# Attention's two passes taken in turns between heads, on key tiles of their own, and the convolution's edge columns copied on ScalarE

## The chip, the core and the metric

The kernel runs on one core of one Trainium2 chip. The metric is the device time of one execution in microseconds (us), lower is better; the time before is the median of three runs. Engines are named as the profile names them: PE (TensorE, matrix products), PEld (its weight loads), DVE (VectorE), ACT (ScalarE), POOL (GpSimd) and SP (SyncE, whose queue issues most DMAs). PE accumulates in PSUM; everything else works on SBUF tiles or on PSUM banks.

## The reference

One block over 2048 tokens with a model width of 1024, all in float32. Shortened:

```python
h = rms_norm(x, norm_mix_g)
z = h @ w_in                          # u_a, v_a (512 each), q, k, v (512 each), 8 forget logits
out_a = spatial_gating(gelu(u_a), gelu(v_a), ...)      # 128-token blocks
c = cumsum(log_sigmoid(f_logit))                       # per head
s = q @ k.T / 8 + c[t] - c[s]         # 8 heads of 64, s <= t
out_b = softmax(s) @ v
x = x + concat(out_a, out_b) @ w_out
a = rms_norm(x, norm_ffn_g) @ w_up    # 2 x 2816 channels
a = causal_conv3(a, w_conv) + b_conv  # depthwise, over tokens
g, val = split(a)
x = x + (silu(g) * val) @ w_down
out = rms_norm(x, norm_final_g)
```

## The kernel before, in words

**Precision and tiling.** A float32 operand is split into a high part, rounded to the matmul's format (fp32r), and a low part (the difference). A product is then three matmuls: high x high, high x low, low x high (`mm3`, recorded at L212; 24 matmuls of 512 columns for a sum over 1024). The high part of a weight is made by POOL (L151), the low part by DVE (L165). Tokens go in blocks `tb` of 512, two blocks to a half of 1024.

**Stages.** Phase A makes q, k, v, the forget sums and the gated heads. `c_half` multiplies by W_out for the first half, `d_half` does the first half's up-projection and convolution (22 pairs of channel tiles, `f`), `c_late` is W_out for the second half, and then the second half's up-projection and both down-projections follow, in another scheme of products. What `c_half` and `c_late` read of attention has gone through DRAM: `b_mix` writes two heads at a time to `mixh` and `mixl`, and `load_mix(blk)` reads a block of 512 tokens back in eight DMAs, into tiles of the tpool that `d_half` uses for its own input. `load_mix(2)` is issued near the end of `d_half`, `load_mix(3)` in the first part of `c_late`.

**Attention** is a generator, `b_stream`, that runs through 32 pieces: token block 0 to 3, and in each the heads 0 to 7. A piece has two passes. `b_max(h, tb)` makes the scores with queries on the partitions (L777, one matmul of 96 rows) and reduces each to its row minimum on DVE (L780, or L782 on the diagonal), since q was stored negated. `b_mix(h, tb)` makes the scores again with keys on the partitions (L824, L828, and a mask at L826), takes exp on ACT into `e` (L830), splits it into `ph` (ACT, L835) and `pl` (DVE, L836), adds it to `sum` (DVE, L838), and multiplies both parts by v into the PSUM bank `o` (L812, L813; "PV" below). Then come the row sums (L854, L855), and after every odd head the normalisation: `rw` (ACT), its four transposes (L186), `op` (DVE, L863), a split and two DMAs to `mixh` and `mixl`. Each `yield` of the generator is one step: one score matmul with its reduction in `b_max`, one chunk of 128 keys in `b_mix`.

**What sets the order.** Attention fills the other stages: `tick` is called after each matmul of the main work, and after `rate` of them (3.6 in `d_half`) one step of attention is written, with a raised priority. `need(tb)` runs the generator on until a token block is done. From all of this a scheduler makes one fixed order for every engine and every DMA queue; on the chip each engine follows its order and waits on semaphores. `b_stream` writes, for each piece, the whole of `b_max(h, tb)` and then the whole of `b_mix` of the piece before:

```python
t1, turn = yield from self.b_max(h, tb)
if todo:
    yield from self.b_mix(*todo, turn)
    self.done += 1
...
todo = (h, tb, t1, self.b_low(h, tb))
```

`t1` holds q's high part with the forget and maximum rows, `m1` the same for the keys, `m2` and `t2` the rest, `v4` the values. Two `m1` buffers are shared by both passes (`b_keys`); `t2` and `sum` have one buffer each. `turn`, a transpose (L796) and a product on DVE (L797), puts the row maxima into `t1`; it is called at the fourth chunk of the mix before. After the first two channel pairs of `d_half` the pool of `c_half`'s rows is closed and `bx` is opened in its place; `more` is true from there to the end of attention, and `room` then gives some tiles (`e`, `ph`, `pl`, `m2`, `v`) further buffers, marked `+`.

**The convolution** in `d_up`: `a` has 514 columns, two of them from the block before. ACT copies the product from PSUM to columns 2 to 513 (L934) and makes `t` from it with the third tap and the bias (L935); DVE copies the two columns from `halo` to `a` (L936) and the last two of `a` to `halo` (L937), and adds the other two taps (L938, L939).

Of the kernel before, what the change touches and what calls it, by code (L numbers as in the profile page):

```python
# [8 lines left out]
F32 = mybir.dt.float32  # L9
F32R = mybir.dt.float32r  # L10
BF16 = mybir.dt.bfloat16
AF = mybir.ActivationFunctionType
ALU = mybir.AluOpType
# [5 lines left out]
P = 128  # L19
# [16 lines left out]
LAG = 2  # L36
TURN = 3
# [16 lines left out]
def f32(ap):  # L54
    return ap.bitcast(F32)
# [26 lines left out]
class Block:  # L82
# [625 lines left out]
    def b_stream(self, pieces):  # L708

        todo = None  # L710
        for h, tb in pieces:
            if tb >= 2 and not self.ready:
                if todo:
                    yield from self.b_mix(*todo, None)
                    self.done += 1
                    todo = None
                while not self.ready:
                    yield
            t1, turn = yield from self.b_max(h, tb)
            if todo:  # L720
                yield from self.b_mix(*todo, turn)
                self.done += 1
            else:
                turn()
            todo = (h, tb, t1, self.b_low(h, tb))
        yield from self.b_mix(*todo, None)
        self.done += 1

# [14 lines left out]
    def b_keys(self, h, sb, values):  # L743
        hf, sl = sb // 2, slice((sb % 2) * TB, (sb % 2 + 1) * TB)
        self.M1.append(self.M1.pop(0))
        m1 = self.M1[0]
# [9 lines left out]
    def b_low(self, h, tb):  # L756

        t2 = self.til(self.mp, [P, TB], F32R, "t2")
        self.dma(f32(t2), self.qx[tb // 2][h, :, (tb % 2) * TB:(tb % 2 + 1) * TB])
        return t2  # L760
# [41 lines left out]
    def b_mix(self, h, tb, t1, t2, turn):  # L802

        nc, bp, pp = self.nc, self.bp, self.bpp
        po = self.til(pp, [P, TB], F32, "o")
        total = self.til(self.mp, [P, TB], F32, "sum")
# [116 lines left out]
    def d_up(self, f, wg, wv, b):  # L923
# [3 lines left out]
        for ch, (wh, wl) in ((f, wg), (NF + f, wv)):  # L927
# [8 lines left out]
            nc.vector.tensor_copy(a[:, 0:2], self.halo[:, ch, :])  # L936
            nc.vector.tensor_copy(self.halo[:, ch, :], a[:, TB:TB + 2])  # L937
            nc.vector.scalar_tensor_tensor(t, a[:, 1:TB + 1], self.cw1[:, cc], t, op0=ALU.mult, op1=ALU.add)  # L938
            nc.vector.scalar_tensor_tensor(t, a[:, 0:TB], self.cw0[:, cc], t, op0=ALU.mult, op1=ALU.add)  # L939
# [14 lines left out]
    def d_half(self):  # L954

        units = lambda f: [self.load_unit(self.a["w_up"][c], P) for c in (f, NF + f)]
        for f0 in range(0, NF, 2):
# [17 lines left out]
            if not f0:  # L975
# [3 lines left out]
                self.more = True  # L979
    def d_sums(self, i):  # L980
# [581 lines left out]
```

## Time and profile before

| | us |
|---|---|
| median of three runs (2420.01 to 2422.13) | 2421.57 |
| the profiled execution, its own time | 2422.66 |
| its span, from the first to the last instruction | 2420.9 |
| PE busy in the span | 2379.3 |
| DVE busy | 1881.9 |
| ACT busy | 1152.9 |
| POOL busy | 331.3 |

The mean granted TensorE clock is 0.995 of full speed. A matmul's record covers its way through the array, so that records overlap: a matmul of 512 columns is shown with some 0.39 us and the next one starts 0.23 us later. What PE loses is therefore read from the starts of its instructions and from its waits. In the rows of a timeline stand the start, the duration, the engine, line, operation, tiles and shapes, and in brackets the idle time before it with what ended it. In the rows of waits stand the total, the count and the longest. In the rows of groups stand the busy time and the mean duration in ns, then the idle time before them.

### The profile page before, as it was taken

The numbers are of one execution on the slowest core, as the hardware profiler recorded it, in microseconds if no ns is written. First come the engines' busy times: TensorE is split into PE (matmuls) and PEld (weight loads), VectorE is DVE, ScalarE is ACT, GpSimd is POOL, SyncE is SP. The second block draws the span as 40 slices with busy tenths as digits, with TensorE's granted clock in tenths as the row PEclk, the third lists the DMA queues.
The fourth block names the chain that finished last, engine by engine and source line by source line (L and its number), as shares of the span: only waits on it lengthen the run. The fifth ranks groups of instructions, "written<-read, shape, count | busy, mean of one in ns | idle before, by whom it ended". The sixth has DMA issues, their size and how long they took to land.

```text
span 2420.9 us, 32633 instructions
## 1 busy us (share of the span) xinstructions
PE 2379.3 (98%) x11352; PEld 1973.2 (82%) x11352; DVE 1881.9 (78%) x3196; ACT 1152.9 (48%) x1987; POOL 331.3 (14%) x315
## 2 busy tenths in 40 slices
PE   9999999999999999999999999899999999999998
PEld 7888878988787888888878888688888888888887
DVE  5457776776579888998999988598888877857775
ACT  4335655533334444454544445465555455454444
POOL 4014140010232222222221110100000000000001
PEclk9999999999999999999999999899999999999999
DMA  8662625567754444444443464312222228438633
GB/s 278 184 230 94 197 74 171 153 188 247 244 193 151 154 142 153 147 140 158 160 155 121 159 217 152 122 53 95 79 81 85 87 93 313 159 98 296 205 119 123
DMA packets 234518, 379.58 MB, mean 157 GB/s; under 512 B 49944, under 2 KB 109464, under 8 KB 232928
## 3 DMA queue, kind: packets, MB, share of 16 engines
q1 hardware_dynamic: 229312, 353.36, 44.9%
q0 software_dynamic: 5040, 24.12, 2.6%
q8 instruction: 90, 1.47, 0.3%
q14 instruction: 76, 0.62, 0.1%
HBM read 283.82 MB, written 93.72 MB: 156 GB/s over the span
## 4 chain that ended last, share of the span: by engine, by line
PE 79%; DVE 5%; DMA 2%; issue 2%; ACT 2%; POOL 1%; SPq 0%; POOLq 0%; DVEq 0%; ACTq 0%
PE mm L212 35%; PE D L1376 13%; PE A L1174 3%; PE A L1176 3%; PE A L1175 3%; PE o L813 3%; PE o L812 2%; PE s L777 2%; PE s L828 2%; PE s L824 2%; PE B L1175 2%; PE B L1176 2%; PE B L1174 2%; PE C L1174 1%; PE C L1175 1%
## 5 line engine op out<-in xcount | busy, mean ns | idle before, releaser
L212 PE MATMUL mm<-thi,wlo 128*128 128x512 f32 x896 | 352.9, 394 | 0.0
L212 PE MATMUL mm<-thi,whi 128*128 128x512 f32 x896 | 352.1, 393 | 0.5 <-DVE vn L520 0.5
L212 PE MATMUL mm<-tlo,whi 128*128 128x512 f32 x896 | 352.5, 393 | 0.0
L212 PE MATMUL mm<-whi,thi 128*128 128x512 f32 (+2 forms) x768 | 277.4, 362 | 14.3 <-DMA thi<-mixh 8.8
L212 PE MATMUL mm<-wlo,thi 128*128 128x512 f32 (+2 forms) x768 | 276.7, 361 | 1.9 <-DVE wlo L165 1.8
L212 PE MATMUL mm<-whi,tlo 128*128 128x512 f32 (+2 forms) x768 | 275.4, 360 | 1.3 <-DMA tlo<-mixl 1.3
L151 POOL TENSOR_SCALAR whi<-raw 128x1024 fp32r<-128x1024 f32 (+3 forms) x114 | 135.2, 1187 | 909.3 <-PE mm L212 665.9
L212 PEld LDWEIGHTS mm<-thi,whi 128*128 128x128 f32 x896 | 168.8, 188 | 34.5 <-issue 0.9
L212 PEld LDWEIGHTS mm<-tlo,whi 128*128 128x128 f32 x896 | 168.8, 188 | 33.9
L212 PEld LDWEIGHTS mm<-thi,wlo 128*128 128x128 f32 x896 | 168.9, 188 | 33.2
L838 DVE TENSOR_TENSOR sum<-sum,e 128x512 f32<-128x512 f32 (+3 forms) x249 | 163.6, 657 | 20.8 <-ACT e L830 18.2
L212 PEld LDWEIGHTS mm<-whi,thi 128*128 128x128 f32 x768 | 146.1, 190 | 35.8 <-DMA thi<-mixh 9.6
L212 PEld LDWEIGHTS mm<-wlo,thi 128*128 128x128 f32 x768 | 146.1, 190 | 22.5 <-DVE wlo L165 3.1
L212 PEld LDWEIGHTS mm<-whi,tlo 128*128 128x128 f32 x768 | 146.0, 190 | 21.4 <-DMA tlo<-mixl 1.7
L830 ACT ACTIVATE e<-s 128x512 f32<-128x512 f32 (+3 forms) x207 | 105.9, 518 | 114.0 <-PE s L828 64.1
L165 DVE TENSOR_TENSOR wlo<-raw,whi 128x1024 fp32r<-128x1024 f32 (+2 forms) x106 | 134.8, 1274 | 28.0 <-POOL whi L151 27.6
L1376 PE MATMUL D<-wh,xh 128*128 128x512 f32 x368 | 140.8, 389 | 1.2 <-DVE xo L1477 1.2
L1376 PE MATMUL D<-wl,xh 128*128 128x512 f32 x368 | 141.4, 389 | 0.0
L836 DVE TENSOR_TENSOR pl<-e,ph 128x512 fp32r<-128x512 f32 (+3 forms) x195 | 122.2, 632 | 20.5 <-PE o L813 10.7
L1376 PE MATMUL D<-wh,xl 128*128 128x512 f32 x368 | 137.5, 389 | 0.0
L835 ACT ACTIVATE ph<-e 128x512 fp32r<-128x512 f32 (+3 forms) x195 | 104.4, 547 | 42.4 <-PE o L812 29.5
L934 ACT ACTIVATE a<-mm 128x512 f32<-128x512 f32 x88 | 52.4, 596 | 119.5 <-PE mm L212 119.1
(1839 smaller groups left out, 5776.2 us busy)
## 6 DMA issues: line engine op xcount, KB each, us to landing
raw<-in_w_up_dram SPq DMA_DIRECT2D x72, 512.0 KB
m<-kx SPq DMA_DIRECT2D x160, 136.0 KB
x<-act SPq DMA_DIRECT2D x84, 256.0 KB
m<-kx SPq DMA_DIRECT2D x67, 256.0 KB
v<-vd SPq DMA_DIRECT2D x67, 256.0 KB
raw<-in_w_in_dram SPq DMA_DIRECT2D x28, 512.0 KB
raw<-in_w_out_dram SPq DMA_DIRECT2D x24, 512.0 KB
tw<-in_w_down_dram SPq DMA_DIRECT2D x11, 1024.0 KB
```

What stands on the lines that cost most here:

```text
L151: self.cast_ins = self.nc.gpsimd.tensor_scalar(out, in_, 1.0, 0.0, ALU.mult, ALU.add).ins
L165: nc.vector.tensor_tensor(lo, raw, f32(hi), op=ALU.subtract)
L212: self.last_mm = self.nc.tensor.matmul(ps, lhsT=a[k], rhs=b[k], start=i == 0, stop=i == 3 * n - 1).ins
L813: nc.tensor.matmul(po[:, c], lhsT=v, rhs=pl[:, c], start=False, stop=sc == ns - 1)
L830: nc.scalar.activation(e[:, c], ps[:, c], AF.Exp, scale=-1.0)
L835: nc.scalar.activation(ph[:, c], e[:, c], AF.Copy)
L836: nc.vector.tensor_tensor(pl[:, c], e[:, c], f32(ph[:, c]), op=ALU.subtract)
L838: nc.vector.tensor_tensor(total[:, c], total[:, c], e[:, c], op=ALU.add)
L1174: mm(ps, lhsT=xh[:, ks], rhs=yh[:, k, :], start=fresh and k == 0, stop=False, **kw)
L1175: mm(ps, lhsT=xh[:, ks], rhs=yl[:, k, :], start=False, stop=False, **kw)
L1176: mm(ps, lhsT=xl[:, ks], rhs=yh[:, k, :], start=False, stop=k == 3, **kw)
L1376: nc.tensor.matmul(bank[t], lhsT=x[i][:, ts], rhs=w[k], start=fresh and j == 0 and i + k == 0, stop=last and i == 1, **kw)
```

## The change

`b_stream` alternates the two passes once `more` is true: three steps of `b_max` of the next head, then two steps of `b_mix` of the one before, until `b_max` is through; the rest of `b_mix` follows, with `turn` called at its fourth remaining step. The mix pass takes its `m1` tiles from a ring of their own (`M1b`, two tiles in the pool `bx`, filled with their constant rows by four memsets on POOL), and `t2` and `sum` get a second buffer there. `b_low`, the load of `t2`, moves from the end of the mix before into the beginning of `b_mix`. In `d_up` both copies of edge columns go from DVE to ACT; for the first block (b = 0), where the edge is zero, the copy into `a` is left out and the two taps run on 511 and 510 columns.

```diff
--- before.py
+++ after.py
@@ -34,6 +34,7 @@
 AHEAD_B, AHEAD_W = 100, 2000
 WARM = 24
 LAG = 2
+FIRST, SECOND = 3, 2
 TURN = 3
 GATE_LAG = 30
 
@@ -43,7 +44,7 @@
     "x": 4, "st": 4, "ln": 2, "vn": 4, "u": 2, "lns": 8, "fs": 7, "fr": 3,
     "m1": 2, "t1": 2, "m2": 2, "v": 2, "t2": 1, "e": 3, "op": 1, "ph": 2, "pl": 2, "part": 2, "mx": 2, "m8": 2,
     "rr": 2, "rw": 1, "sum": 1,
-    "ar": 4, "a": 2, "t": 4, "ss": 4, "rs": 4, "rstd": 8, "tw": 1, "s0": 1, "va": 2, "e+": 1, "ph+": 2, "pl+": 2, "m2+": 1, "v+": 1,
+    "ar": 4, "a": 2, "t": 4, "ss": 4, "rs": 4, "rstd": 8, "tw": 1, "s0": 1, "va": 2, "e+": 1, "ph+": 2, "pl+": 2, "m2+": 1, "v+": 1, "m1+": 2, "sum+": 1, "t2+": 1,
     "mm": 2, "tp": 2, "dn": 2, "s": 3, "o": 1,
     "y": 1, "sf": 2, "tq": 1, "cv": 2, "ts": 2, "xgP2l": 1, "xgP2h": 1, "xgP1l": 1, "xgP1h": 1, "xsP7l": 1, "xsP7h": 1, "xsP6l": 1, "xsP6h": 1, "xsP5l": 1, "xsP5h": 1, "xsP4l": 1, "xsP4h": 1, "xsP3l": 1, "xsP3h": 1, "pc": 2, "A": 3, "B": 1, "C": 3,
     "wr": 2, "wh": 3, "wl": 3, "xh": 3, "xl": 3, "x11": 9, "wr+": 2, "wh+": 2, "wl+": 2, "xh+": 2, "xl+": 2, "x11+": 2, "x12": 11, "x21": 11, "x22": 11, "xs": 2,
@@ -716,15 +717,44 @@
                     todo = None
                 while not self.ready:
                     yield
-            t1, turn = yield from self.b_max(h, tb)
-            if todo:
-                yield from self.b_mix(*todo, turn)
+            if todo and self.more:
+                first, second = self.b_max(h, tb), self.b_mix(*todo, None)
+                t1 = None
+                while t1 is None:
+                    for _ in range(FIRST):
+                        t1, turn = yield from self.one(first)
+                        if t1 is not None:
+                            break
+                    if t1 is None:
+                        for _ in range(SECOND):
+                            yield from self.one(second)
+                for n, _ in enumerate(second):
+                    if n == TURN:
+                        turn()
+                        turn = None
+                    yield
+                if turn:
+                    turn()
                 self.done += 1
             else:
-                turn()
-            todo = (h, tb, t1, self.b_low(h, tb))
+                t1, turn = yield from self.b_max(h, tb)
+                if todo:
+                    yield from self.b_mix(*todo, turn)
+                    self.done += 1
+                else:
+                    turn()
+            todo = (h, tb, t1)
         yield from self.b_mix(*todo, None)
         self.done += 1
+
+    def one(self, gen):
+
+        try:
+            next(gen)
+        except StopIteration as end:
+            return end.value or (None, None)
+        yield
+        return None, None
 
     def room(self, shape, dt, tag):
 
@@ -742,8 +772,9 @@
 
     def b_keys(self, h, sb, values):
         hf, sl = sb // 2, slice((sb % 2) * TB, (sb % 2 + 1) * TB)
-        self.M1.append(self.M1.pop(0))
-        m1 = self.M1[0]
+        ring = self.M1b if values and self.more else self.M1
+        ring.append(ring.pop(0))
+        m1 = ring[0]
         self.dma(f32(m1[0:68, :]), self.kx[hf][h, 64:132, sl])
         if not values:
             return m1
@@ -755,7 +786,7 @@
 
     def b_low(self, h, tb):
 
-        t2 = self.til(self.mp, [P, TB], F32R, "t2")
+        t2 = self.room([P, TB], F32R, "t2")
         self.dma(f32(t2), self.qx[tb // 2][h, :, (tb % 2) * TB:(tb % 2 + 1) * TB])
         return t2
 
@@ -799,11 +830,12 @@
 
         return t1, turn
 
-    def b_mix(self, h, tb, t1, t2, turn):
+    def b_mix(self, h, tb, t1, turn):
 
         nc, bp, pp = self.nc, self.bp, self.bpp
+        t2 = self.b_low(h, tb)
         po = self.til(pp, [P, TB], F32, "o")
-        total = self.til(self.mp, [P, TB], F32, "sum")
+        total = self.room([P, TB], F32, "sum")
         ns = 4 * tb + 4
         late = []
 
@@ -933,10 +965,13 @@
             cc = slice(ch, ch + 1)
             nc.scalar.activation(a[:, 2:TB + 2], ps, AF.Copy)
             nc.scalar.activation(t, ps, AF.Identity, scale=self.cw2[:, cc], bias=self.cb[:, cc])
-            nc.vector.tensor_copy(a[:, 0:2], self.halo[:, ch, :])
-            nc.vector.tensor_copy(self.halo[:, ch, :], a[:, TB:TB + 2])
-            nc.vector.scalar_tensor_tensor(t, a[:, 1:TB + 1], self.cw1[:, cc], t, op0=ALU.mult, op1=ALU.add)
-            nc.vector.scalar_tensor_tensor(t, a[:, 0:TB], self.cw0[:, cc], t, op0=ALU.mult, op1=ALU.add)
+            if b:
+                nc.scalar.activation(a[:, 0:2], self.halo[:, ch, :], AF.Copy)
+            nc.scalar.activation(self.halo[:, ch, :], a[:, TB:TB + 2], AF.Copy)
+            for n, cw in ((1, self.cw1), (0, self.cw0)):
+                c = slice(0 if b else 2 - n, TB)
+                nc.vector.scalar_tensor_tensor(t[:, c], a[:, n + c.start:n + TB], cw[:, cc], t[:, c],
+                                               op0=ALU.mult, op1=ALU.add)
             outs.append(t)
             if ch == f:
                 spare = a
@@ -977,6 +1012,11 @@
                 self.accs.close()
                 self.bx = self.bxs.enter_context(self.tc.tile_pool(name="bxpool", bufs=1, side="right", reuse_waits="tile"))
                 self.more = True
+                self.M1b = [self.til(self.bx, [P, TB], F32R, "m1+") for _ in range(2)]
+                for m in self.M1b:
+                    self.nc.gpsimd.memset(f32(m[64:128, :]), 0.0)
+                    self.nc.gpsimd.memset(f32(m[96:104, :]), 1.0)
+
     def d_sums(self, i):
 
         nc, dp = self.nc, self.dp
```

What that does to the fixed order is seen at three places. The names are those of the tiles above, with the scheduler's numbers; line numbers after the change are larger by 1 in `mm3` and by 31 to 32 in attention and the convolution.

PE, at the end of attention, where the last head of token block 3 is finished. Before:

```order
L813 MATMUL o_13295<-pl_13582,v_13528 128x256
L812 MATMUL o_13295<-ph+_3163_13597,v_13528 128x128
L854 MATMUL s_13625<-mhalf,sum_13296 128x1
L813 MATMUL o_13295<-pl+_3164_13598,v_13528 128x128
L186 MATMUL dn_13636<-ident,rw_13631 128x128 x4
L212 MATMUL mm_15087<-whi_14883,thi_14853 128x512
L212 MATMUL mm_15087<-wlo_14884,thi_14853 128x512
```

After:

```order
L213 MATMUL mm_14538<-thi_7659,whi_14333 128x512
L213 MATMUL mm_14538<-tlo_7661,whi_14333 128x512
L845 MATMUL o_13271<-pl_13557,v_13504 128x256
L844 MATMUL o_13271<-ph+_3165_13572,v_13504 128x128
L845 MATMUL o_13271<-pl+_3166_13573,v_13504 128x128
L213 MATMUL mm_14538<-thi_7659,wlo_14334 128x512
L213 MATMUL mm_14538<-thi_7659,whi_14333 128x512
```

Before, the last PV (L813) is followed at once by the transposes of `rw` and then by products of W_out on the tiles that `load_mix(3)` fills with the attention heads. After, the last PV (L845) stands in the middle of the up-projection's last products (L213 on `thi` and `whi`): 22 more L213 rows, the four transposes of `rw`, and 225 further L213 rows follow before the next transposes. Counted over PE's whole order, 4836 of the 4992 L212 rows stand ahead of the last attention matmul before, and 4538 after; the up-projection ends at 4608.

DVE, in the middle of `d_half`, where the max pass of head 1 of token block 3 meets the mix pass of head 0. Before:

```order
L936 COPY a_12747<-halo 128x2
L780 TENSOR_REDUCE part_9779<-s_9878 128x1
L780 TENSOR_REDUCE part_9779<-s_9885 128x1
L938 SCALAR_TENSOR_TENSOR t_12604<-a_12605,cols,t_12604 128x512
L780 TENSOR_REDUCE part_9779<-dn_9856 128x1
L939 SCALAR_TENSOR_TENSOR t_12604<-a_12605,cols,t_12604 128x512
L780 TENSOR_REDUCE part_9779<-dn_9872 128x1
L950 TENSOR_TENSOR va_12406<-t_12486,t_12604 128x512
L936 COPY a_12823<-halo 128x2
L937 COPY halo<-a_12747 128x2
```

After:

```order
L870 TENSOR_TENSOR sum_9816<-sum_9816,e_9837 128x512
L811 TENSOR_REDUCE part_9772<-s_9862 128x1
L973 SCALAR_TENSOR_TENSOR t_11952<-a_11953,cols,t_11952 128x511
L870 TENSOR_TENSOR sum_9816<-sum_9816,e_9871 128x512
L811 TENSOR_REDUCE part_9772<-s_9906 128x1
L868 TENSOR_TENSOR pl_9840<-e_9837,ph_9839 128x512
L811 TENSOR_REDUCE part_9772<-s_9913 128x1
L973 SCALAR_TENSOR_TENSOR t_11952<-a_11953,cols,t_11952 128x510
L868 TENSOR_TENSOR pl+_2240_9874<-e_9871,ph+_2239_9873 128x512
L870 TENSOR_TENSOR sum_9816<-sum_9816,e_9894 128x512
```

Before, the reductions of the max pass (L780) follow each other with only the convolution (L936 to L939, L950) between them, and no row of a mix pass. After, each reduction (L811) stands between rows of the mix pass (`sum`, L870, and `pl`, L868) and of the convolution (L973), and the copies of 2 columns are gone.

ACT, where it takes a product of the up-projection out of PSUM. Before:

```order
L934 ACTIVATE a_11568<-mm_11446 128x512
L935 ACTIVATE t_11567<-mm_11446,cols 128x512
L946 ACTIVATE a_11568<-t_11567 128x512
L830 ACTIVATE e_9103<-s_9100 128x512
L830 ACTIVATE sum_9082<-s_9088 128x512
L835 ACTIVATE ph_9105<-e_9103 128x512
```

After:

```order
L966 ACTIVATE a_11682<-mm_11561 128x512
L967 ACTIVATE t_11681<-mm_11561,cols 128x512
L969 ACTIVATE a_11760<-halo 128x2
L970 ACTIVATE halo<-a_11682 128x2
L862 ACTIVATE e_9688<-s_9684 128x256
```

The two copies of 2 columns (L969, L970) now stand on ACT behind the two readings of the product, and ahead of the exp (L862) of the next chunk.

## The prediction

> **What bounds the kernel now.** I read the page's first part, then busy time by stretches, then PE's waits, and last PE's own timeline and the chain of waits around the one place where PE stands still.
>
> ```profile
> PE 2379.3 (98%) x11352; PEld 1973.2 (82%) x11352; DVE 1881.9 (78%) x3196; ACT 1152.9 (48%) x1987; POOL 331.3 (14%) x315
> core 0: us, PE busy (x) PEld busy (x) DVE busy (x) ACT busy (x) POOL busy (x), PEclk, DMA share, GB/s
> 200.00:720.00 520.00, 512.77 (x2726) 430.17 (x2725) 375.00 (x700) 237.25 (x396) 103.24 (x82) 1.00 0.57 175
> 780.00:1512.00 732.00, 730.36 (x3389) 599.19 (x3387) 652.44 (x1202) 354.47 (x647) 132.30 (x112) 1.00 0.47 156
> 1512.00:1530.00 18.00, 8.93 (x37) 6.80 (x37) 5.09 (x9) 10.16 (x15) 3.49 (x8) 0.62 0.56 203
> 1530.00:1560.00 30.00, 30.00 (x143) 24.90 (x143) 16.52 (x24) 8.68 (x14) 5.46 (x7) 1.00 0.26 90
> ```
>
> PE is busy for 98% of the span, so whatever the change frees on DVE is worth nothing by itself. Most of the change acts between 780 and 1512 us, the first half's up-projection with attention filled in. PE idles there for 1.64 of 732 us, although DVE is at 89% (652.44 of 732). The next 18 us are the exception: PE is busy for 8.93 us, at a mean clock of 0.62.
>
> ```profile
> 1512.49 0.31 PE L813 MATMUL o<-pl+_3164_13598,v 128*128 128x128 f32 x1
> 1514.13 0.94 PE L186 MATMUL dn<-ident,rw 128*128 128x128 f32 x4 [1.33 <-ACT rw L860]
> 1522.37 0.80 PE L212 MATMUL mm<-whi,thi 128*128 128x512 f32 x1 [7.30 <-DMA thi<-mixh]
> 1522.96 0.63 PE L212 MATMUL mm<-wlo,thi 128*128 128x512 f32 x1
> ...
> 1527.65 1.21 PE L186 MATMUL dn<-ident,ar 128*128 128x128 f32 x8
> 1529.30 1.16 PE L186 MATMUL dn<-ident,ar 128*128 128x128 f32 x8 [0.44 <-DVE ts L1026]
> 1530.41 0.50 PE L212 MATMUL mm<-whi,thi 128*128 128x512 f32 x1
> ...
> 1530.98 0.40 PE L212 MATMUL mm<-whi,tlo 128*128 128x512 f32 x1
> 1531.21 0.39 PE L212 MATMUL mm<-whi,thi 128*128 128x512 f32 x1
> ```
>
> ```profile
> 1515.11 0.70 DVE op L863
> 1515.83 0.64 ACT ph+_3168_13642 L199
> 1516.49 1.96 DMA mixh<-ph+_3168_13642
> 1518.47 3.86 DMA thi<-mixh
> ```
>
> This is attention's handover to W_out. The last PV matmul (L813) starts at 1512.49. The last two heads must be normalised, split, written to mixh and read back before the W_out product of the last 512 tokens can finish, and PE has nothing else left. Start times tell the price: between 1512.49 and 1530.41 stand one 128-column matmul, 4 + 16 transposes and 12 L212. At full clock an L212 starts 0.23 us after the one before it (1530.98 to 1531.21), and eight transposes take 0.79 us, as these two rows show.
>
> ```profile
> 1535.31 1.03 PE L186 MATMUL dn<-ident,ar 128*128 128x128 f32 x8
> 1536.10 0.48 PE L212 MATMUL mm<-whi,thi 128*128 128x512 f32 x1
> ```
>
> So the work is 0.06 + 20 x 0.099 + 12 x 0.227 = 4.8 us, done in 17.9: **13.1 us are lost**, some 9 of them idle and the rest at the lower clock.
>
> **The change, part by part.** (1) The alternation, with m1, t2 and sum on buffers of their own, leaves the fill rate and the number of steps as they were. What it does to the order is seen on PE at the end of attention, which in the order printed above comes 298 L212 rows earlier: 4538 of the 4992 L212 rows stand ahead of it in place of 4836. It now lies 70 rows ahead of the end of the up-projection, and 265 PE rows ahead of the first that reads any tile of load_mix(3). That is about 60 us at 0.227, where the chain above needs 1512.49 to 1522.37, 9.9 us. The gap goes whole, and with it the lower clock: **-13.1 us**. Bounds: 0 if the wait only moves, -13.1 if it goes.
>
> At the lower clock, L212 starts lie 0.59 us and then 0.43 apart. The Trainium skill, "TensorE: Matmul & The Clock Gate", Part 1 on the clock gate, says that the clock halves after an idle window of about 3.4 us and comes back after a busy one. The trace agrees: 7.30 us idle, then PEclk 0.62. By that rule a remainder over 3.4 us would keep an estimated 1.7 us of slow work beside itself and a shorter one none, which changes only the partial rival below.
>
> (2) What is late next in 780 to 1512? These are PE's only waits there, below them the longest of their kinds in the whole run, and last SP's longest wait in the stage:
>
> ```profile
> PE o L813 <- DVE pl+_2522_11042 L836: 1.1, 1, 1.1
> PE o L813 <- DVE pl L836: 0.4, 1, 0.4
> ...
> PE mm L212 <- DMA thi<-mixh: 8.8, 2, 7.3
> PE o L813 <- DVE pl L836: 4.5, 4, 2.8
> PE mm L212 <- DMA tlo<-mixl: 1.3, 1, 1.3
> PE s L777 <- DMA t<-cc: 0.9, 1, 0.9
> ...
> SPq L101 <- PE s L777: 97.4, 24, 11.3
> ```
>
> Ten heads' mix passes are alternated (counted in the order). In each, a PV waits for e, ph and pl of its own chunk; between two chunks now stand one or two reductions of the next head (L780) on DVE, and as many scores and several L212 on PE. That gives each chain more time than four L836/L838 in a row had. Bounds: -1.5 us (both waits go) to +28 (one wait of 2.8 us in each of ten heads). I take 0, since the nearest rows are these two waits in 732 us.
>
> (3) t2's load moves on SP's queue from the end of the mix before to the first step of its own, behind t1's two loads and a key tile of the next head's max, and m2 and v stand behind it. The second t2 buffer lets it start while the mix before still reads the other; a separate m1 ring keeps max's loads from waiting for mix's readers. Bounds: 0 to +9 (ten heads at the 0.9 us that t<-cc cost once); taken 0. Before the extra pool opens, t2 has one buffer and stands a row or so later; the scheduler reshuffles phase A and the first W_out stage a little. PE idles there for 7.2 us between 200 and 720; I allow 3 either way and take 0.
>
> (4) With attention gone, the start of the late W_out stage (first 512 tokens) has no filler, so its load_mix(2), eight 512 KB transfers, must be in time. In before they move in this stretch:
>
> ```profile
> 1386.13 0.36 SPq L101 DMA_DIRECT2D tlo<-mixl  x1
> 1391.58 0.48 SPq L101 DMA_DIRECT2D tlo<-mixl  x1
> ...
> 1386.00:1392.00 6.00, 6.00 (x29) 4.95 (x28) 4.32 (x12) 1.90 (x3) 0.00 (x0) 1.00 0.75 268
> 1392.00:1398.00 6.00, 6.00 (x28) 4.99 (x27) 4.78 (x13) 1.27 (x2) 1.05 (x1) 1.00 1.05 350
> 1398.00:1404.00 6.00, 6.00 (x28) 4.87 (x28) 4.95 (x8) 5.08 (x11) 1.05 (x1) 1.00 0.75 261
> ```
>
> 4.2 MB at those rates are there by about 1401, 15 us. In the new order 119 PE rows (some 25 us) lie between the last reader of those buffers and the first W_out matmul. Covered, by about 10 us. If not, the price is that of the same stage earlier, 1.5 + 1.3 us; taken **+0.6**, a fifth of it, for the thin cover.
>
> (5) The edge columns. In 780 to 1512:
>
> ```profile
> L939 DVE SCALAR_TENSOR_TENSOR t<-a,cols,t 128x512 f32<-128x512 f32 x82 | 67.9, 828 | 0.6
> L938 DVE SCALAR_TENSOR_TENSOR t<-a,cols,t 128x512 f32<-128x512 f32 x82 | 64.8, 790 | 4.8 <-ACT t L935 4.7
> L936 DVE COPY a<-halo 128x2 f32<-128x2 f32 x81 | 27.9, 344 | 0.2
> L937 DVE COPY halo<-a 128x2 f32<-128x2 f32 x82 | 15.7, 192 | 16.2 <-ACT a L934 16.0
> ...
> L1228 ACT ACTIVATE cv<-halo x22: 187/206/221, 1589.5 to 1974.6; 128x4 f32<-128x4 f32 x22
> ACT a L934 <- PE mm L212: 111.2, 45, 6.2
> ```
>
> DVE loses 43.6 us of copies there, and its 16 us wait for ACT at L937 mostly moves to L938. ACT gains 132 copies, by L1228's 0.206 us some 27 us, beside 111 us in which it waited for matmuls at L934. On PE's path: 0, and if the cover were gone, 0.2 us before a PSUM bank that the next product needs 5 us later. The 44 + 44 rows of 511 and 510 columns change nothing.
>
> The Trainium skill, "VectorE: DVE Perf Modes", its section on the TRN2 errata, speaks against this part: a SBUF copy has a fixed cost of 224 cycles on ScalarE and 58 on VectorE. By it (an estimate) ACT gains 25 us and DVE loses 11, not 44; the rows (206 ns on ACT, means of 344 and 192 on DVE) show a larger relief, and the sum is 0 either way.
>
> (6) Four memsets on POOL for the new m1 tiles, on an engine busy for 132 of 732 us: 0.
>
> **Sum.** -13.1 + 0.6 = -12.5. The profiled execution took 2422.66 us (span 2420.9 and 1.8 around it), so 2410.2; the median of the three runs is 1.1 lower, so **2409.0**.
>
> **Rivals.** *The gap shrinks but part comes back* (14%), as late loads in (4) or as waits in (2) and (3), for instance half of the ten heads at 0.9 us (4.5) and 2.8 in (4): 2408.5 + 7.3 = 2416, range 2414 to 2420. For it: SP serves its queue in order and 97 us of its time there go to waiting for scores. Against it: the counts of rows above.
>
> *The change doesn't do what it says on the chip* (8%): the order has attention early, but DVE cannot keep that pace, and PE waits in small pieces for what it waited for in one. Then about 2421.6. For it: 298 L212 rows at 0.227 are 68 us, so the same attention has 732 - 68 = 664 us. DVE's 652 us lose 0 to 44 in copies and, with 12.4 groups of 24 L212, up to 20 in their L938 and L939 (1.62 us a group): 588 to 652, that is 89 to 98%. Against it: even that stays under 100%, and at 89% PE idled for 1.6 us.
>
> *Slower* (7%): at the upper end of that DVE share a reduction stands in front of each pl, and PE waits at L813 once in every alternated head as long as the longest such wait, 2.8 us: +28 - 13.1, so 2436. It decides from the point at which DVE's work between two PV rows exceeds PE's, a DVE share above 100% in a head; from 1.3 us a head on, the gain is gone.
>
> **How the numbers follow.** The forecast, 2404 to 2414, has 71%. The range leaves out most of the last two: 2403 to 2419. A measurement can tell 0.2%, 4.8 us: faster means under 2416.7. That is the forecast and most of the first rival, 0.80; the same 0.13; slower 0.07.
>
> **What would show it.** In the profile after: no PE wait for mixh near the end of attention, PEclk 1.00 there, the last L813 some 60 us earlier; in the alternated stage PE waits of a few us in all, and DVE's share at 98% at most; ACT copies near 0.2 us. Wrong would be: a wait of PE of over 3 us at the first late W_out product, or many waits of about 1 us at L845 or for t2.

## The result and the profile after

| | before | after |
|---|---|---|
| median of six runs, us | 2421.32 (2419.90 to 2423.31) | 2401.68 (2400.76 to 2402.74) |
| the profiled execution, its own time | 2422.66 | 2402.74 |
| its span | 2420.9 | 2401.0 |

The ratio of the times is 0.9919, with a 95% interval of 0.9906 to 0.9932: the changed kernel is faster by 19.6 us. The forecast was 12.5 us less than before, 2409.0, with a range of 2403 to 2419; 2401.68 lies below it. The direction was right, the size was not, and the runs below show that the prediction looked for the cause in the wrong part of the change.

Busy time of PE, PEld, DVE, ACT and POOL by stretches, with PEclk, DMA share and GB/s at the end of a row, for the changed kernel:

```profile
660.00:668.00 8.00, 8.00 (x41) 6.44 (x40) 4.36 (x10) 1.38 (x2) 0.00 (x0) 1.00 0.34 117
726.00:734.00 8.00, 8.00 (x42) 6.51 (x41) 7.71 (x9) 1.80 (x4) 4.42 (x4) 1.00 0.80 289
780.00:1455.00 675.00, 671.41 (x3112) 550.22 (x3111) 600.54 (x1003) 357.37 (x750) 126.14 (x105) 1.00 0.46 152
1512.00:1530.00 18.00, 18.00 (x85) 14.97 (x85) 11.76 (x16) 4.28 (x8) 4.23 (x3) 1.00 0.20 59
```

Where PE stood still at 1512 to 1530 it now works for 18.00 of 18.00 us at full clock. The end of attention on PE's timeline of the changed kernel:

```profile
1438.90 0.28 PE L845 MATMUL o<-pl+_3166_13573,v 128*128 128x128 f32 x1
1439.01 0.45 PE L213 MATMUL mm<-thi,wlo 128*128 128x512 f32 x1
...
1444.08 0.60 PE L187 MATMUL dn<-ident,rw 128*128 128x128 f32 x4
1444.44 0.48 PE L213 MATMUL mm<-thi,whi 128*128 128x512 f32 x1
```

The last PV matmul (L845) starts at 1438.90, 73.6 us earlier than before (1512.49): 298 rows at 0.227 us make 67.6 of them, and time won earlier the rest. The transposes of `rw` follow 5 us later between products of the up-projection, without a wait. The 13.1 us of the handover are gone whole.

But 13.1 is not 19.9, the difference of the two profiled executions. The rest lies 850 us earlier, at a place that the prediction passed over. From PE's timeline of the kernel before, with the idle time ahead of a row and what ended it in brackets, then its clock in the two stretches that meet at the third row, and two rows of DVE's timeline there:

```profile
663.67 0.50 PE L212 MATMUL mm<-whi,thi 128*128 128x512 f32 x1 [1.48 <-DMA thi<-mixh]
667.00 0.50 PE L212 MATMUL mm<-whi,tlo 128*128 128x512 f32 x1 [1.35 <-DMA tlo<-mixl]
...
729.48 0.80 PE L813 MATMUL o<-pl,v 128*128 128x512 f32 x1 [2.80 <-DVE pl L836]
...
732.91 0.39 PE L212 MATMUL mm<-tlo,whi 128*128 128x512 f32 x1
...
779.05 0.50 PE L813 MATMUL o<-pl,v 128*128 128x512 f32 x1 [1.03 <-DVE pl L836]
```

```profile
726.00:729.48 3.48, 0.68 (x4) 0.22 (x3) 3.48 (x4) 0.02 (x1) 3.09 (x3) 0.97 0.24 67
729.48:732.70 3.22, 3.22 (x10) 2.63 (x11) 3.22 (x8) 2.60 (x6) 0.47 (x1) 0.50 1.00 331
```

```profile
725.45 2.31 DVE L165 TENSOR_TENSOR wlo<-raw,whi 128x1024 fp32r<-128x1024 f32 x1 [0.94 <-POOL whi L151]
727.68 1.74 DVE L836 TENSOR_TENSOR pl<-e,ph 128x512 fp32r<-128x512 f32 x1
```

The first two rows are the same handover once more, for the first half: `c_half` waits for the attention heads of token block 1 to come back from DRAM (1.48 + 1.35). The waits for `pl` that follow are no handover. The one of 2.80 us is that of the seventh of twelve PVs of token block 2's first head, whose `pl` stands on DVE behind the split of a weight (`wlo`, L165) that had waited for POOL; the one of 1.03 us lies in the second head. Behind the 2.80 us the clock is at 0.50; from 729.48 to 732.91 stand six matmuls of 512 columns and four transposes, 6 x 0.227 + 4 x 0.099 = 1.8 us of work in 3.4, so 1.7 more are lost. Together **8.3 us**. In the changed kernel PE is busy for 8.00 of 8.00 us from 660 to 668 and from 726 to 734, at clock 1.00 (rows above). Its waits from 595 to 1560 us (total, count, longest):

```profile
PE tq L187 <- DVE cv L1066: 1.3, 1, 1.3
PE s L808 <- issue: 1.2, 1, 1.2
PE o L845 <- DVE pl L868: 1.1, 2, 0.6
PE s L808 <- DMA m<-kx: 0.9, 1, 0.9
PE s L860 <- DMA t<-qx: 0.5, 1, 0.5
PE s L187 <- ACT rw L892: 0.4, 1, 0.4
```

13.1 + 8.3 = 21.4. The new waits among these rows, and a stretch at half clock behind one of them (last section), take some of it back; what is left up to 19.9 lies in small differences elsewhere and is not traced here.

### The profile page after: what moved, and what is told of

It is laid out like the page before. It is cut to its first block, busy times and chain, and to the rows that moved or that the text cites. A ratio compares the mean times of both kernels' runs of the same rounds, so it can differ in the third digit from the quotient of the medians.

```text
span 2401.0 us, 32528 instructions
## 1 busy us (share of the span) xinstructions
PE 2372.6 (99%) x11352; PEld 1971.0 (82%) x11352; DVE 1843.7 (77%) x3020; ACT 1162.8 (48%) x2117; POOL 331.3 (14%) x319
## 4 chain that ended last, share of the span: by engine, by line
PE 81%; DVE 4%; issue 2%; DMA 2%; ACT 1%; POOL 1%; SPq 0%; POOLq 0%; DVEq 0%; ACTq 0%
PE mm L213 36%; PE D L1416 14%; PE A L1214 3%; PE A L1216 3%; PE A L1215 3%; PE o L845 2%; PE o L844 2%; PE s L860 2%; PE s L808 2%; PE s L856 2%; PE B L1216 2%; PE B L1215 2%; PE B L1214 2%; PE C L1214 1%; PE C L1215 1%
## 5 line engine op out<-in xcount | busy, mean ns | idle before, releaser
L213 PE MATMUL mm<-thi,whi 128*128 128x512 f32 x896 | 352.9, 394 | 2.5 <-DVE vn L521 2.5
L213 PE MATMUL mm<-thi,wlo 128*128 128x512 f32 x896 | 354.1, 395 | 0.0
L213 PE MATMUL mm<-tlo,whi 128*128 128x512 f32 x896 | 353.1, 394 | 0.0
L213 PE MATMUL mm<-whi,thi 128*128 128x512 f32 (+2 forms) x768 | 275.9, 360 | 6.2 <-DVE vn L521 5.9
L213 PE MATMUL mm<-wlo,thi 128*128 128x512 f32 (+2 forms) x768 | 275.3, 359 | 1.6 <-DVE wlo L166 1.6
L213 PE MATMUL mm<-whi,tlo 128*128 128x512 f32 (+2 forms) x768 | 274.8, 358 | 0.0
L213 PEld LDWEIGHTS mm<-thi,whi 128*128 128x128 f32 x896 | 169.1, 189 | 36.4 <-issue 2.8
L213 PEld LDWEIGHTS mm<-thi,wlo 128*128 128x128 f32 x896 | 168.9, 189 | 34.2
L213 PEld LDWEIGHTS mm<-tlo,whi 128*128 128x128 f32 x896 | 169.0, 189 | 33.8
L213 PEld LDWEIGHTS mm<-whi,thi 128*128 128x128 f32 x768 | 145.4, 189 | 26.3 <-DVE vn L521 6.1
L213 PEld LDWEIGHTS mm<-wlo,thi 128*128 128x128 f32 x768 | 145.4, 189 | 22.1 <-DVE wlo L166 2.3
L213 PEld LDWEIGHTS mm<-whi,tlo 128*128 128x128 f32 x768 | 145.3, 189 | 19.9
L862 ACT ACTIVATE e<-s 128x512 f32<-128x512 f32 (+3 forms) x208 | 106.6, 520 | 110.0 <-PE s L860 88.2
L973 DVE SCALAR_TENSOR_TENSOR t<-a,cols,t 128x512 f32<-128x512 f32 (+2 forms) x176 | 143.7, 817 | 13.1 <-ACT t L967 12.0
L868 DVE TENSOR_TENSOR pl<-e,ph 128x512 fp32r<-128x512 f32 (+3 forms) x195 | 124.0, 640 | 20.6 <-PE o L845 15.4
L870 DVE TENSOR_TENSOR sum<-sum,e 128x512 f32<-128x512 f32 (+3 forms) x189 | 120.0, 635 | 20.9 <-ACT e L862 17.8
```

Of the source, the lines that this page charges most:

```text
L213: self.last_mm = self.nc.tensor.matmul(ps, lhsT=a[k], rhs=b[k], start=i == 0, stop=i == 3 * n - 1).ins
L862: nc.scalar.activation(e[:, c], ps[:, c], AF.Exp, scale=-1.0)
L868: nc.vector.tensor_tensor(pl[:, c], e[:, c], f32(ph[:, c]), op=ALU.subtract)
L870: nc.vector.tensor_tensor(total[:, c], total[:, c], e[:, c], op=ALU.add)
L973: nc.vector.scalar_tensor_tensor(t[:, c], a[:, n + c.start:n + TB], cw[:, cc], t[:, c], op0=ALU.mult, op1=ALU.add)
```

## The experiments

A count is used in all of them: how many of the 4992 main matmuls (`mm3`, 0.227 us each) stand in PE's fixed order ahead of the last PV matmul of attention. It is 4836 before and 4538 after. At 4836 the next main matmul needs the attention heads of token block 3, so that a kernel with 4836 has the handover, and one with N has (4836 - N) x 0.227 us for its chain of 9.9 us. The theory at the start was: the time went with the handover at 1512 and with the waits near 663 to 730 us. The rivals were that the relief of DVE by the edge copies is worth the rest, or that the alternation itself removes waits all through the stage.

| kernel | count | median us | before beside it | ratio and 95% interval |
|---|---|---|---|---|
| e_alt_only | 4578 | 2400.58 | 2420.75 | 0.9913, 0.9900 to 0.9927 |
| e_edge_only | 4836 | 2421.16 | 2420.75 | 1.0001, 0.9992 to 1.0010 |
| e_noalt | 4755 | 2398.53 | 2420.75 | 0.9904, 0.9890 to 0.9917 |
| e_m1_shared | 4836 | 2426.85 | 2420.75 | 1.0023, 1.0014 to 1.0032 |
| e_t2_only | 4760 | 2401.37 | 2421.12 | 0.9923, 0.9911 to 0.9936 |
| e_t2_early | 4590 | 2409.12 | 2421.12 | 0.9952, 0.9939 to 0.9964 |
| e_noalt_edge | 4820 | 2407.13 | 2421.12 | 0.9942, 0.9929 to 0.9954 |
| e_bufs | 4836 | 2422.54 | 2421.12 | 1.0006, 0.9997 to 1.0015 |
| e_x3 | 4836 | 2424.94 | 2422.30 | 1.0008, 0.9999 to 1.0017 |
| e_x3_t2x2 | 4756 | 2405.37 | 2422.30 | 0.9926, 0.9913 to 0.9938 |
| e_t2_edge | 4760 | 2403.80 | 2422.30 | 0.9919, 0.9906 to 0.9933 |
| e_noalt_r37 | 4726 | 2402.18 | 2422.30 | 0.9913, 0.9900 to 0.9927 |
| e_after_again | 4538 | 2402.19 | 2420.95 | 0.9919, 0.9905 to 0.9932 |
| e_noalt_again | 4755 | 2398.84 | 2420.95 | 0.9909, 0.9895 to 0.9922 |
| e_t2_only_again | 4760 | 2401.58 | 2420.95 | 0.9918, 0.9904 to 0.9931 |

### The edge copies: e_alt_only and e_edge_only

The first puts the two copies of the changed kernel back on DVE, the second puts only them on ACT in the kernel before, with the shorter taps of the first block.

```diff
-            if b:
-                nc.scalar.activation(a[:, 0:2], self.halo[:, ch, :], AF.Copy)
-            nc.scalar.activation(self.halo[:, ch, :], a[:, TB:TB + 2], AF.Copy)
...
+            nc.vector.tensor_copy(a[:, 0:2], self.halo[:, ch, :])
+            nc.vector.tensor_copy(self.halo[:, ch, :], a[:, TB:TB + 2])
```

> The changed kernel with the edge columns copied on VectorE again, as before the change (the alternation and the buffers stay). In its fixed order the last attention matmul has 4578 main matmuls ahead of it, 258 fewer than before the change. Theory (the time went with the handover and with waits of the attention stream, the edge copies are worth nothing): within 2 us of the changed kernel's 2401.7. Rival (the 7 us beyond the forecast come from the 44 us that VectorE lost in copies): 2407 to 2410.

> The kernel before with only the edge columns copied on ScalarE. The end of attention stays where it was (4836 main matmuls ahead). Theory: 2421 within 3 us, with the wait for mixh of about 7 us at the end of attention still there. Rival (relief of VectorE is worth the 7 us): 2413 to 2415.

Measured: 0.9913 without the copies on ACT, beside 0.9919 with them, and 1.0001 with them alone. In e_edge_only DVE is busy for 1850.0 us in place of 1881.9, and PE's waits from 595 to 1560 us still hold both handovers (three of the rows):

```profile
PE mm L212 <- DMA thi<-mixh: 8.4, 2, 7.5
PE o L813 <- DVE pl L836: 5.5, 4, 3.6
PE mm L212 <- DMA tlo<-mixl: 1.3, 1, 1.3
```

The copies by themselves are worth nothing; that rival falls.

### Without the alternation, and the alternation on shared key tiles: e_noalt and e_m1_shared

```diff
-            if todo and self.more:
-                first, second = self.b_max(h, tb), self.b_mix(*todo, None)
...
-            else:
-                t1, turn = yield from self.b_max(h, tb)
+            t1, turn = yield from self.b_max(h, tb)
+            if todo:
+                yield from self.b_mix(*todo, turn)
```

> The changed kernel without the alternation: the two passes of a head one after the other as before, but with t2 loaded at the start of its own mix pass, with its own m1 tiles, second t2 and sum buffers, and the edge copies on ScalarE. The last attention matmul has 4755 main matmuls ahead, 81 fewer than before the change, some 18 us at 0.227 us each, where the chain of the handover took 9.9. Theory (only the place of the end counts, and the waits near 663 to 730 us went with the moved t2 load): the gap goes without any alternation, 2402 to 2406. Rival (the alternation itself removes waits all through the stage): 2409 or more.

```diff
-        ring = self.M1b if values and self.more else self.M1
+        ring = self.M1
```

> The changed kernel with the two m1 tiles shared by both passes again (the alternation, the second t2 and sum and the edge copies on ScalarE stay). The last attention matmul is back at 4836 main matmuls. Theory (only the place of the end counts): the gap of 13 us stays, the 4 to 5 us won before the extra pool opens stay won: 2416 to 2419. Rival (the alternation is worth it by itself): 2402 to 2408; a third outcome is over 2421, if two passes in turn fight for two m1 tiles and TensorE waits for their loads.

Without its title part the change is as fast as with it: 2398.5, lower than expected. The alternation on two shared m1 tiles is slower than before, and the theory's 2416 to 2419 missed it; the third outcome came, over 2421. PE's waits from 595 to 1560 us in e_m1_shared, three of the largest five:

```profile
PE mm L213 <- DMA thi<-mixh: 7.5, 1, 7.5
PE s L856 <- DMA m<-kx: 3.1, 3, 1.5
PE dn L856 <- DMA m<-kx: 1.4, 1, 1.4
```

The large handover is back (7.5) and the first one is not (the wait for `mixh` is there once, not twice). PE also waits 4.5 us for key tiles (`m<-kx`). So the alternation on shared tiles puts the end of attention back to 4836, and it needs tiles of its own to make attention early. Without any alternation attention is early too (4755), so something else in the change does that. What is left is the moved load of t2 and the second buffers.

### The moved load: e_t2_only, e_t2_early, e_bufs, e_noalt_edge

e_t2_only is the kernel before with this edit alone:

```diff
-            todo = (h, tb, t1, self.b_low(h, tb))
+            todo = (h, tb, t1)
...
-    def b_mix(self, h, tb, t1, t2, turn):
+    def b_mix(self, h, tb, t1, turn):
...
+        t2 = self.b_low(h, tb)
```

> The kernel before with one edit: t2 is loaded at the start of its own mix pass and no longer at the end of the mix pass before (t2 keeps its one buffer; no alternation, no further m1, t2 or sum tiles, edge copies on VectorE). In the fixed order every head of attention ends 40 to 95 main matmuls earlier than before the change, from the first half's keys on, and the last at 4760 in place of 4836 of 4992: 76 rows, 17 us, against the 9.9 us of the handover's chain. Theory (the moved load is what counts): 2400 to 2406. Rival (the second buffers are needed for it): 2410 or more.

e_t2_early is the changed kernel with exactly this edit taken back.

> The changed kernel with t2 loaded at the old place, at the end of the mix pass before (alternation, own m1 tiles, second t2 and sum and the edge copies on ScalarE stay). The last attention matmul has 4590 main matmuls ahead, far from the handover, so the alternation too can remove that gap. Theory (the handover's 13 us go, the 4 to 5 us of waits near 663 to 730 us stay, since there nothing differs from the kernel before): 2404 to 2408. Rival (without the moved load the handover comes back or TensorE waits for t2 in the alternated heads): 2412 or more.

e_bufs gives the kernel before the own m1 ring and `room` for t2 and sum, and nothing else.

> The kernel before with own m1 tiles for the mix pass and second t2 and sum buffers, and nothing else of the change. The last attention matmul stays at 4836. Theory (buffers alone move nothing): 2418 to 2423, with the wait for mixh of about 7 us still there. Rival (freeing the m1 tiles and t2 lets attention's loads run early enough): 2412 or less.

e_noalt_edge is e_noalt with the copies on DVE, which happens to end attention at 4820.

> The kernel before with t2 loaded in its own mix pass, own m1 tiles for the mix pass and second t2 and sum buffers; no alternation, edge copies on VectorE. The last attention matmul has 4820 main matmuls ahead: 16 rows, 3.6 us, before the first that needs the written-back heads, where the chain takes 9.9. Theory (the place of the end decides): some 6 us of the gap stay, with part of the low clock, 2404 to 2410. Rival (the place does not matter, the moved load alone does): 2398 to 2401, as without the alternation but with the copies on ScalarE.

The three moved lines alone give 2401.4, the time of the whole change. The buffers alone give nothing (1.0006). The changed kernel without the moved load gives 2409.1, just above what was expected of it. PE's waits from 595 to 1560 us, first e_t2_only (all of them), then three rows of e_t2_early, then the first row of e_noalt_edge:

```profile
PE tq L186 <- DVE cv L1027: 1.3, 1, 1.3
PE o L814 <- DVE pl+_2284_10067 L837: 1.0, 1, 1.0
PE o L814 <- DVE pl L837: 1.0, 2, 0.6
PE o L814 <- DVE pl+_2792_12132 L837: 0.2, 1, 0.2
```

```profile
PE o L844 <- DVE pl L867: 3.7, 2, 3.6
PE mm L213 <- DMA thi<-mixh: 1.5, 1, 1.5
PE mm L213 <- DMA tlo<-mixl: 1.2, 1, 1.2
```

```profile
PE mm L213 <- DMA thi<-mixh: 5.2, 1, 5.2
```

With the moved load alone neither handover is left. In e_t2_early the alternation has removed the second one and the first stands as before (1.5 and 1.2 for `mixh` and `mixl`), as does the wait for `pl` behind it (3.6): both lie ahead of the place where the alternation begins. That the wait for `pl` goes with the moved load is shown; which shift in the order removes it is not. The 2409.1 of e_t2_early against the changed kernel's 2401.7 is 7.4 us, where the rows above gave 8.3. In e_noalt_edge the count of 4820 leaves 16 x 0.227 = 3.6 us for a chain of 9.9; 6.3 should be missing, and PE waits for 5.2. So the place of the end does decide, and the edge copies can shift it, as they do between e_noalt and e_noalt_edge (8.6 us), though they cost nothing themselves.

### Why the load matters: e_x3 and e_x3_t2x2

SP's fixed order at the start of one head's max pass, the loads of `t1` (64 rows), `t2` (128 rows, 256 KB), the two further rows of `t1` (`cc`) and the first key tile (68 rows). Before:

```
L101 DMA t_50_404<-qx_74 64x512
L101 DMA t_1724_7743<-qx_74 128x512
L101 DMA t_50_404<-cc_78 2x512
L101 DMA m_48_402<-kx_75 68x512
```

With the moved load:

```
L101 DMA t_50_404<-qx_74 64x512
L101 DMA t_50_404<-cc_78 2x512
L101 DMA m_48_402<-kx_75 68x512
L101 DMA t_1751_7890<-qx_74 128x512
```

None of these is issued before the mix pass before has made its last score, which reads `t2`'s one buffer and the one of `t1`'s two that comes next. The first score of the max pass needs `t1`, `cc` and the key tile; it doesn't need `t2`, whose load stood ahead of two of the three. On the chip, PE's rows in the kernel before, and of the same head with the moved load alone:

```profile
850.71 0.31 PE L828 MATMUL s<-t,m 128*128 128x128 f32 x1
...
857.31 0.40 PE L777 MATMUL s<-m,t 96*128 96x512 f32 x1
```

```profile
829.59 0.31 PE L829 MATMUL s<-t,m 128*128 128x128 f32 x1
...
835.81 0.70 PE L777 MATMUL s<-m,t 96*128 96x512 f32 x2
```

From the last score of one pass (L828, L829) to the first of the next (L777) it takes 6.6 us before and 6.2 with the moved load. PE does not wait there, it works on main matmuls; so the step is one of the fixed order, not a wait on the chip. Nor is it shorter in every head: of 28 such steps in the two traces, 17 are shorter with the moved load and 11 longer (medians 7.5 and 6.5 us). The place of the heads' ends is surer. How many main matmuls stand ahead of a head's row sums in PE's fixed order:

| token block, head | before | e_bufs | e_t2_only | e_x3_t2x2 | e_t2_early | after | e_noalt |
|---|---|---|---|---|---|---|---|
| 1, 7 | 2246 | 2246 | 2201 | 2202 | 2246 | 2201 | 2201 |
| 2, 0 | 2534 | 2534 | 2487 | 2487 | 2534 | 2487 | 2487 |
| 2, 7 | 3686 | 3681 | 3629 | 3629 | 3583 | 3513 | 3607 |
| 3, 3 | 4301 | 4310 | 4224 | 4224 | 4121 | 4067 | 4211 |
| 3, 7 | 4836 | 4836 | 4756 | 4755 | 4583 | 4528 | 4750 |

With the moved load alone 45 rows of lead are there by the end of token block 1, ahead of the extra pool, and 80 at the end. In e_t2_early the alternation adds its own lead from token block 2 on.

Does the place of the line in the code matter, or only where the load stands in SP's queue? With two t2 buffers from the beginning the load stays at its old place in the code, but need not wait, and the scheduler puts it behind the key tile too. For its space x has one buffer less, which the control shows alone:

```diff
-    "x": 4, "st": 4, "ln": 2,
+    "x": 3, "st": 4, "ln": 2,
...
-    "v": 2, "t2": 1, "e": 3,
+    "v": 2, "t2": 2, "e": 3,
```

> A control for the next run: the kernel before with three buffers in place of four for phase A's input tile x, which frees the space of one t2. The order of attention is that of before, every head from token block 2 on at the same count of main matmuls, the last at 4836. Both theories: 2419 to 2425.

> As the control, and t2 with two buffers from the beginning, its load at the old place, at the end of the mix pass before. Theory (what cost the time is that the load waits at the old place for the last reader of the one buffer, with the next head's loads of t1 and m1 behind it in SP's queue; a second buffer lifts that as well as the move does): every head ends where it does with the moved load, the last at 4756, and the time is that of the moved load alone, 2400 to 2404 (plus what the control costs over before). Rival (the place of the load itself counts, between which other loads it stands): 2412 or more.

It comes out as the theory has it: the heads end where they do with the moved load (the columns of e_x3_t2x2 and e_t2_only agree to 1), and the ratio is 0.9926 beside 0.9923, with a control at 1.0008. The two kernels have in common that t2's load no longer stands ahead of `cc` from the third head on, and they don't tell a wait for the buffer from the time of the load itself.

But that place in the queue is not enough in the late heads. In e_bufs t2 has its second buffer once the extra pool is open, and there too SP takes t2 last, for the last ten heads. The first of these, in the kernel before (the first row holds the loads of `t1` and `t2`) and in e_bufs:

```profile
960.80 1.08 SPq L101 DMA_DIRECT2D t<-qx  x2
961.93 0.29 SPq L101 DMA_DIRECT2D t<-cc  x1
962.26 0.65 SPq L101 DMA_DIRECT2D m<-kx  x2
```

```profile
960.01 0.45 SPq L101 DMA_DIRECT2D t<-qx  x1
960.50 0.44 SPq L101 DMA_DIRECT2D t<-cc  x1
960.99 0.71 SPq L101 DMA_DIRECT2D m<-kx  x2
961.74 0.43 SPq L101 DMA_DIRECT2D t<-qx  x1
```

The last ten steps from one pass to the next are then 6.4 us shorter in sum than before, and still the heads end near where they did (3681, 4310 and 4836 in the table) and no time is won. So small steps saved late did not add up to an earlier end there. The moved load differs in that it acts from the third head on. How the scheduler makes the lead of 45 to 80 rows out of that is not shown.

### What more could be had: e_t2_edge, e_noalt_r37, and three side by side

e_t2_edge is e_t2_only with the copies on ACT. e_noalt_r37 is e_noalt with `RATES = [3.5, 4.0, 4.4, 3.7]` in place of 3.6.

> The kernel before with t2 loaded in its own mix pass and the edge columns copied on ScalarE; one t2, one sum, two m1 tiles, no alternation. The last attention matmul has 4760 main matmuls ahead, as with the moved load alone. Theory (with the end of attention out of the way the copies are worth nothing on either engine): 2398 to 2402, that is within 3 us of the moved load alone. Rival (the copies are worth 3 us and more once the handover is gone, as the kernel without alternation at 2398.5 may say): 2396 to 2398.

> The changed kernel without the alternation (2398.5), and attention filled into the up-projection at 3.7 main matmuls a step in place of 3.6. The last attention matmul has 4726 main matmuls ahead in place of 4755, since the fixed order follows no simple rule there. Theory (beyond some 10 us of lead an earlier end is worth nothing): 2397 to 2400. Rival (the earlier end still pays, since the last small matmuls of attention move off the W_out stage): 2394 to 2396.

Both expectations were missed by 2 us on the slow side; the intervals of the two ratios (0.9919 and 0.9913) still reach into what was expected. A lead of 110 rows (4836 - 4726, 25 us) is not seen to be worth more than one of 76.

> The changed kernel once more, on the same chip as the next two. Theory and rival: 2400 to 2403.

> The changed kernel without the alternation once more, beside the changed kernel. Theory (with the moved load in place the alternation adds nothing, the 3 us between the two medians so far lie within what differs from chip to chip): within 2 us of the changed kernel. Rival (the alternation costs some 3 us, since between 780 and 1455 us the changed kernel waits for key tiles, t2 and pl with a short stretch of low clock at 1211): 2.5 to 4 us below the changed kernel.

> The kernel before with the moved load alone once more, beside the changed kernel. Theory (the one moved load is worth the whole change): within 2 us of the changed kernel. Rival (the rest of the change is worth something on top): 3 us or more above it.

The moved load alone (2401.58) and the whole change (2402.19) are the same. The change without the alternation (2398.84) lies 3.3 us lower, and lay 3.1 below the changed kernel's first median in its first run (2398.53), but its interval (0.9895 to 0.9922) overlaps that of the whole change (0.9905 to 0.9932). That the alternation costs something may be and is not shown; that it gains nothing here is shown. e_noalt has the lowest median of the versions that were run.

## Why the prediction was right and wrong, point by point

**The bound and the gap at 1512.** Right. The 13.1 us were lost as counted, and they are gone whole, with the clock back at 1.00 and the last PV 73.6 us earlier, where some 60 were said.

**Step 1, the alternation moves the end of attention: -13.1.** Right in size, and not the cause that matters. With the moved load taken back, the rest of the change gives 2409.1, which is the forecast of 2409.0 nearly to the digit, and by the mechanism that was forecast. But the same gap goes with the moved load alone, so that in the changed kernel the handover is removed twice over.

**Step 3, the moved load of t2: taken 0, bounds 0 to +9, and 3 either way ahead of the extra pool.** This is the step that failed. Alone it is worth 2421.12 - 2401.37 = 19.8 us. The prediction saw that the load moves behind t1's two loads and a key tile, and asked only what it would make late (t2 itself), not what it had kept late; its bounds for the alternated heads allowed a loss and no gain. The 0.9 us that it took as the price of a late t2 (`t<-cc`, at 461.58 us) is a first score waiting for `cc`, which SP had issued behind t2. What the runs show in its place: with the load moved, attention is 45 rows earlier at the end of token block 1 and 76 at its own end (4760 in place of 4836), and both handovers are gone. And it gave 3 us either way to the schedule ahead of the pool, where 8.3 us lay; its two stretches, 200 to 720 and 780 to 1512 us, leave out 720 to 780, with 2.80, 1.03 and 1.7 of them. How the scheduler turns the place of one load into that lead stays open.

**The row that held it.** The prediction quoted the wait `thi<-mixh: 8.8, 2, 7.3`: two waits, one of 7.3. It used the 7.3. The other 1.5 and the 1.3 for `mixl` beside it belong to the first half's W_out, and two of the four waits for `pl` (2.8 and 1.0 of 4.5) follow it. The term "what removes the handover" stood for one place, where the kernel hands over twice.

**Step 2, waits in the alternated stage: taken 0, bounds -1.5 to +28.** About right: PE is busy for 671.41 of 675 us, so it idles 3.6 us in place of 1.6; a stretch at half clock comes on top (last section).

**Step 4, cover of load_mix(2): +0.6.** No wait for `thi` or `mixh` is left; the term is 0.

**Step 5, edge copies: 0.** Right (1.0001 alone). DVE's busy time falls by 31.9 us in e_edge_only, between the 11 and the 44 of the prediction. On ACT they take what was said, by the groups of the changed kernel between 780 and 1512 us:

```profile
L970 ACT ACTIVATE halo<-a 128x2 f32<-128x2 f32 x81 | 16.5, 204 | 0.0
L969 ACT ACTIVATE a<-halo 128x2 f32<-128x2 f32 x40 | 8.2, 205 | 0.0
```

24.7 us there, by 0.204 us each, and DVE's share between 780 and 1455 stays at 89% (600.54 of 675), in the 89 to 98% of the second rival. That rival and the slower one did not come. The alternation can cost time, though: e_m1_shared, without key tiles of its own, is at 1.0023, with the handover back and 4.5 us of waits for key tiles.

**The sum.** -13.1 + 0.6 was forecast, -19.6 measured (-19.9 between the profiled executions). The missing term is the place at 663 to 779 us, -8.3, less the new waits.

## What to carry to other kernels

When a gap is found and a change removes it, look for its smaller twins: a wait listed with a count of two is two places. Of a load that moves behind others, ask first what it had stood in front of: here t2 stood ahead of two loads that the next score needed. Read the gain from where each piece ends in the fixed order, early pieces too: steps made shorter late brought no earlier end here. And test the title of a change by leaving it out: here three moved lines did the whole work.

## What had not been expected of the hardware

The clock went to half after pauses shorter than the prediction reckoned with. In the kernel before, 2.80 us of waiting at 729.48 are followed by 3.2 us at 0.50 (rows above). At 1514 the clock is at 0.50 from 1514.30 us on, behind a wait of 1.33 us and ahead of that of 7.30 us which the prediction took for the cause: the four transposes of `rw` at 1514.13 already take 0.94 us, in the changed kernel 0.60. In the profiled execution of the changed kernel one wait of 1.21 us at 1209.64, amid matmuls of one and of 128 columns, is followed by this:

```profile
1208.00:1211.30 3.30, 2.09 (x15) 1.80 (x14) 0.00 (x0) 0.60 (x1) 2.14 (x2) 0.97 0.26 85
1211.30:1214.60 3.30, 3.30 (x9) 2.61 (x8) 3.12 (x2) 0.00 (x0) 3.22 (x3) 0.51 0.04 11
```

PE is busy for 2.09 of 3.30 us, and the next 3.3 us run at 0.51. The Trainium skill, "TensorE: Matmul & The Clock Gate", Part 1, has the clock halved after at least one idle window of about 3.4 us. Here the measurement decides: half clock doesn't need a whole such window without work.

So a price of the clock can come on top of waits of 1 to 3 us too, some 1.7 us as counted at 729. It doesn't come behind every wait of this length: those of 1.48 and 1.35 us at 663 and 667 show none (PEclk 1.00 from 660 to 668). Nor does the same wait always bring it. Two executions of the changed kernel, the one shown so far and that of e_after_again, both wait for 1.98 us ahead of a matmul near 481.6 us, and then run like this:

```profile
481.70:485.10 3.40, 3.39 (x15) 2.85 (x16) 3.06 (x11) 0.54 (x2) 1.05 (x1) 1.00 1.10 355
481.70:485.10 3.40, 3.40 (x9) 2.62 (x10) 3.06 (x10) 0.54 (x2) 1.04 (x1) 0.51 1.12 353
```

The first keeps full clock and the second goes to half. What decides it is not shown here.
